# Four operands of the output projection made ahead in place of six, with the loads of that work four to five slots ahead of their use

## The chip, the cores and the metric

One core of a Trainium2 chip. The metric is the device time of one run of the whole kernel in microseconds; the time before is the median of three runs. The profile is one more execution, with its own time.

## The reference

A decoder layer on x of 2048 positions by 1024 channels, in float32, cut to what matters here:

```python
xn = rms_norm(h, ln_g)
proj = jnp.einsum('bsd,de->bse', xn, w_in)              # 6 groups of 1024 columns
b_gate, c_gate, x_conv, g_conv, x_lru, g_lru = jnp.split(proj, splits, axis=-1)
y_conv = headwise_rms_norm(short_conv_mixer(b_gate, c_gate, x_conv, conv_w), 8, conv_out_g) * silu(g_conv)
y_lru = headwise_rms_norm(rg_lru_mixer(x_lru, ...), 16, lru_out_g) * silu(g_lru)
h = h + jnp.einsum('bse,ed->bsd', jnp.concatenate([y_conv, y_lru], -1), w_out)
return rms_norm(h, final_g)
```

The mixers are a short convolution and a gated linear recurrence (two small matrix products for its gates, then a scan over the positions).

## The kernel before

**Steps.** All matrix work is cut into 64 steps (`steps`, L287), numbered n in the text. Steps 0 to 23 are the input projection for the first 1024 positions, steps 24 to 47 the same for the second 1024: eight triples of l (the recurrence's two column groups), a and b (the convolution's four), 128 columns of each group at a time. Steps 48 to 63 are the output projection: `("o", ph, m)`, where ph 0 takes the recurrence's half of the channels and ph 1 the convolution's, and m = 0 to 7 takes 256 positions. Each step is a product of a small operand S and a big operand T, each cut into two by two blocks, by a scheme of seven block products in place of eight (L225 has their order). Every operand block is split into a high part, rounded to fp32r, and a low part, and a product takes high by high, high by low and low by high. So a product is 4 x 3 matmuls of 128 by 128 by 512, and a step is 84 of them. All matmuls are issued in `mm` (L900).

**T and S.** T stays in SBUF for many steps: a set for each half of the positions, and one for each ph (w_out). Steps 24, 48 and 56 begin with a new T; they do six products interleaved by T's parts as these come in, and their seventh product in the next step. S changes with each step. Seven S tiles of 512 KB go round in a pool (`sp`). S is made by `s_plan` (L179) from four raw blocks: four sums on DVE, seven casts on ACT (`hi`, L200), seven subtractions (`lo`), all on DVE from step 24 on. In the first half the results are also stored in `sd`, and the second half loads them instead (`s_loads`, L218): seven loads of 512 KB a step.

**The output projection's S** is z, the mixers' output with its per-head norm: `load_z` (L300) loads four blocks of yd (raw, 256 KB each) and four of the norms' reciprocal roots (zr, 256 KB each by a broadcast; for ph 0 in two halves of 64 partitions, so 12 transfers, for ph 1 8). Four multiplications on DVE follow in later slots. Called for a step itself, zr lies in the tiles u and r of the recurrence; called for the work below, in four more pieces of the raw pool (8 pieces).

**Work made ahead.** z for the first 1024 positions (m = 0 to 3) is known early in the second half, so the generator `jobs` (L363) makes seven operand tiles for some of the steps `(ph, m)` during steps 30 to 47: it loads z, multiplies, and then makes one operand a slot, a cast on ACT (L421) and a subtraction on DVE into a tile of the pool hl (4 buffers), whose store to `so` (512 KB) is asked two slots later. In between it makes T's sums of w_out: `blocks` loads four raw blocks (1 MB), `sums` and `more` combine them on DVE, and four stores (1 MB) to `td` follow; there are eight such sets. When the step comes, `load_next` (L917) finds it in `made` and loads the seven operands from `so`, or else makes them by `s_plan` from `load_z`.

**Order.** Each engine works off its instructions in the order in which the program writes them. There is no scheduler: a slot begins with `tick` (L151), which runs what `at` put off and one piece of `jobs`; then come the loads and preparations (`prep`) for the next step, then the slot's matmuls. `may` (L352) holds the making back in five slots of each a step and when hl is short. Nearly all transfers are asked on SP, in order; a transfer waits for its buffer, and all behind it wait too. At most eight are under way.

**Loads of the steps.** `load_next(n + 2)` stands in slot 3 of a step (L1177), which is four or five slots ahead of the multiplications. In steps that begin with a new T it stands at their end (L1161), after the preparations that load the first five S tiles of step n + 1, and the multiplications come in the first two slots of that step.

Of the kernel before, what the change touches and what calls it, by code (L numbers as in the profile page):

```python
# [38 lines left out]
def hymba_kernel(ctx: ExitStack, tc: tile.TileContext, x, xt, w_in, par, lamc, w_gate, w_out, final_g, out):  # L39
# [27 lines left out]
    def piece(name):  # L67
        return rawp.tile([P, C], F32, tag="raw", name=name)

    def aux(name):  # L70
        return small.tile([P, C], F32, tag="aux", bufs=4, name=name)
# [72 lines left out]
    def at(slots, *fs):  # L144
        if slots == 0:
            for f in fs:
                f()
        else:
            due.append([slots, fs])
# [12 lines left out]
    def tt(out, a, b, op, eng=None):  # L162
        (eng or nc.vector).tensor_tensor(out=out, in0=a, in1=b, op=op)  # L163
# [188 lines left out]
    def may():  # L352
        p = place[0]
        if 8 <= p <= 12:
            return False
        return hlc[0] < (2 if p >= 20 or p <= 2 else 4)

    def w_blocks(t, j):
        k = j + (3 - t) * KT
        return [w_out[(k + i * NB) * P:(k + i * NB + 1) * P, q * C:(q + 1) * C]  # L360
                for i in range(2) for q in range(2)]

    def jobs():  # L363
        tjobs = [(t, j) for t in (2, 3) for j in range(NB)]
        for ph, m in ((0, 0), (0, 1), (1, 0), (1, 1), (0, 2), (0, 3)):
            (a11, a12, a21, a22), fs = load_z(ph, m, False, None)
            yield
            yield
            for f in fs[:2]:
                f()  # L370
            yield
            for f in fs[2:]:
                f()
            yield
            x_ = aux("s3")
            tt(x_, a11, a21, ALU.subtract)
            tt(a21, a21, a22, ALU.add)
            b = {}

            def blocks():  # L380
                if tjobs:
                    b[0] = tjobs.pop(0)
                    b[1] = [piece("traw") for _ in range(4)]
                    for p, src in zip(b[1], w_blocks(*b[0])):
                        nc.sync.dma_start(p, src)

            def sums():
                if b:
                    b11, b12, b21, b22 = b[1]
                    tt(b11, b12, b11, ALU.subtract)  # L390
                    tt(b12, b22, b12, ALU.subtract)

            def more():
                if b:
                    b11, b12, b21, b22 = b[1]
                    tt(b22, b22, b11, ALU.subtract)
                    tt(b21, b21, b22, ALU.subtract)
                    to = td[b[0]]
                    at(1, lambda: [nc.sync.dma_start(to[n], v) for n, v in enumerate((b22, b11, b12, b21))])
                    b.clear()  # L400

            blocks()
            prev = None
            nothing = lambda: None
            items = [(0, a11, lambda: tt(a11, a21, a11, ALU.subtract)), (3, x_, nothing), (2, a21, nothing),
                     (1, a11, nothing), (4, a12, lambda: tt(a12, a12, a11, ALU.subtract)),
                     (6, a22, nothing), (5, a12, nothing)]
            for n, (i, v, after) in enumerate(items):
                if prev:
                    prev()  # L410
                    prev = None
                if n in (1, 5):
                    sums()
                if n in (2, 6):
                    more()
                if n == 4:
                    blocks()
                while not may():
                    yield
                t, = hl_tile("so")  # L420
                nc.scalar.copy(t[:, 0:C], v)  # L421

                def prev(t=t, i=i, v=v, after=after, dst=so[ph, m]):
                    tt(t[:, C:2 * C], v, t[:, 0:C].bitcast(F32), ALU.subtract)
                    after()
                    at(2, lambda: nc.sync.dma_start(
                        dst[i], t.bitcast(F32).rearrange("p (h c) -> p h c", h=2)))
                    at(3, lambda: hl_done(1))

                yield  # L430
            prev()
            made.add((ph, m))
            yield


    class TParts:
# [105 lines left out]
    sums, summed = [None], [0]  # L542
# [374 lines left out]
    def load_next(n, d=2):  # L917
        if n < N:
            Sn[n] = {}
            kind, h, k = steps[n]  # L920
            src = None
            if kind == "o":
                src = so[h, k] if (h, k) in made else None
            elif h == 1 and k > 0:
                src = sd[3 * k + "lab".index(kind)]
            plan[n] = s_loads(src, Sn[n]) if src is not None else s_plan(n, load_s(n, d), Sn[n])

    def prep(n, s):
        if n < N:
            plan[n][s]()  # L930
# [3 lines left out]
    with tc.manual_schedule(engines={ENG.PE, ENG.Activation, ENG.DVE, ENG.Pool, ENG.SP}):  # L934
# [176 lines left out]
        for n in range(PLAIN, N):  # L1111
# [9 lines left out]
            if jm:  # L1121
                bk = {}
                for j in range(NB):
                    place[0] = 2 * j
                    tick()
                    if j < 3:
                        tick()
                    if j == 0:
                        prep(n, 7)
                    if Tq is not None and j < 3:  # L1130
                        Tq.parts((14, 21, 28)[j])
                    elif j == 0:
                        Tp[0].hi(6)
                        Tp[0].lo(6)
                        load_t(2, Tp[2].r)
                    elif j == 1:
                        load_t(3, Tp[3].r)
                    if Tq is None and j < 3:
                        Tp[j + 1].whole()
                    if j == 2:  # L1140
                        load_next(n + 1, 0)
                    if j == 3:
                        prep(n + 1, 0)
                    for i in ORDER[:6]:
                        if j == 0:
                            bk[i] = bank(s=i == 2)
                        mm(bk[i], S_, T, i, j, j == 0, j == NB - 1)
                q1, u2, rr = sm("q1"), sm("u2"), sm("rr")
                nc.scalar.copy(q1, bk[0])
                prep(n + 1, 1)  # L1150
                prep(n + 1, 2)
                tt(u2, bk[1], q1, ALU.add)
                prep(n + 1, 3)
                tt(rr, bk[2], u2, ALU.add)
                tt(u2, bk[3], u2, ALU.add)
                prep(n + 1, 4)
                put(11, bk[4], q1)
                put(22, bk[3], rr)
                put(12, bk[5], rr)
                prep(n + 1, 5)  # L1160
                load_next(n + 2, 1)  # L1161
                pend = (S_, None, put, u2)
                continue
            bk = {}
            for s in range(8 if new or last else 7):
# [43 lines left out]
                elif nx:  # L1209
                    if soon and s == 5:  # L1210
                        Tq = TParts(nx, T2)
# [86 lines left out]
```

## Time and profile before

| | |
|---|---|
| time, median of 3 runs | 1403.29 us (1401.82 to 1404.75) |
| profiled execution | 1404.29 us, of which the span is 1402.2 us |
| granted clock of TensorE, mean | 0.981 |
| moved by the DMA engines | 371.00 MB, mean 265 GB/s |
| so: stores and loads | 42 and 42, of 512 KB each |
| DMA s<-sd, raw<-yd | 147 of 512 KB, 64 of 256 KB |

The span goes from the first instruction to the last; what the run's time has beyond it lies around it. In the views, PE is the matmul engine, PEld its loading of weights, DVE, ACT, POOL the vector, scalar and general engines, SPq the queue of SP. A row of the busy time by stretches has the stretch in us, its length, then for each engine its busy time and (x) instructions, the granted clock (PEclk, 1.00 is full), the share of the DMA engines' time and what they moved. A row of the chain of waits has the start, the length and what was waited for or worked. A row of the list of waits says who waited, at which line, for whom: us in total, times, longest. Rows of groups have busy time and mean ns, then idle time ahead of them.

### The profile page before, as it was taken

How to read it: one execution, taken by the hardware profiler on the slowest of the kernel's cores; microseconds unless marked ns; L12 is line 12 of the kernel's file. 1: busy time of each engine (PE TensorE's matmuls, PEld its weight loads, DVE VectorE, ACT ScalarE, POOL GpSimd, SP SyncE). 2: the span in 40 equal slices, each digit the busy share in tenths (PEclk: the TensorE clock that was granted, in tenths of full speed). 3: DMA queues.
4: the chain of work that ended last, by engine and by line, in shares of the span. 5: the costliest groups of instructions: out<-in, count | busy, mean ns of one | idle time of the engine just before them, and what ended most of it. 6: DMA issues, size and time to landing. Idle time of an engine off the chain costs nothing.

```text
span 1402.2 us, 16765 instructions
## 1 busy us (share of the span) xinstructions
PE 1309.4 (93%) x5612; PEld 1056.3 (75%) x5612; DVE 1071.1 (76%) x1274; ACT 749.3 (53%) x1135; POOL 225.9 (16%) x160
## 2 busy tenths in 40 slices
PE   6989999999999997899998998999998989989997
PEld 5867777787877775678876876787886868867886
DVE  6778888798989889778677787666649447658885
ACT  7475767566565756375563545354556123344443
POOL 2204233233433330101010110101010000000000
PEclk9999999999999998999999999999999999999999
DMA  5147698888988875631899999989878798698643
GB/s 216 30 142 252 255 284 238 288 321 274 337 289 311 307 259 205 230 112 43 292 374 356 389 350 385 343 275 323 286 278 275 286 297 256 220 403 296 216 153 138
DMA packets 166485, 371.00 MB, mean 265 GB/s; under 512 B 18944, under 2 KB 53760, under 8 KB 166400
## 3 DMA queue, kind: packets, MB, share of 16 engines
q1 hardware_dynamic: 166112, 369.63, 76.1%
q8 instruction: 44, 0.72, 0.2%
q14 instruction: 41, 0.34, 0.1%
q10 hardware_dynamic: 288, 0.32, 0.1%
HBM read 224.45 MB, written 145.43 MB: 264 GB/s over the span
## 4 chain that ended last, share of the span: by engine, by line
PE 43%; DMA 19%; DVE 14%; ACT 6%; issue 6%; SPq 2%; POOL 1%; DVEq 0%; ACTq 0%; POOLq 0%
PE bank L900 42%; DMA s<-so 3%; DMA zr<-rsd 3%; DVE s L163 3%; DMA sd<-s 3%; DMA yd<-gl 2%; DVE sums L586 2%; PE gate L680 2%; ACT i L687 2%; ACT r L687 1%; DMA traw<-td 1%; DMA so<-so 1%; DVE u L654 1%; DMA raw<-in_w_in_dram 1%; DMA s<-sd 1%
## 5 line engine op out<-in xcount | busy, mean ns | idle before, releaser
L900 PE MATMUL bank<-th,s 128*128 128x512 f32 x3608 | 1142.2, 395 | 47.8 <-ACT q L1234 12.6
L900 PEld LDWEIGHTS bank<-th,s 128*128 128x128 f32 x3608 | 685.8, 190 | 207.9 <-ACT q L1234 15.6
L900 PE MATMUL bank<-tl,s 128*128 128x512 f32 x1804 | 710.7, 394 | 10.2 <-DVE tl L163 9.9
L900 PEld LDWEIGHTS bank<-tl,s 128*128 128x128 f32 x1804 | 343.0, 190 | 86.4 <-DVE tl L163 15.2
L163 POOL TENSOR_TENSOR s<-raw,s 128x512 fp32r<-128x512 f32 x62 | 110.3, 1791 | 251.3 <-ACT s L200 221.1
L1237 ACT COPY u<-bank 128x512 f32<-128x512 f32 x58 | 34.0, 587 | 168.6 <-PE bank L900 69.6
L200 ACT CAST s<-raw 128x512 fp32r<-128x512 f32 x136 | 82.1, 616 | 64.1 <-PE bank L900 44.2
L163 DVE TENSOR_TENSOR tl<-traw,th 128x512 fp32r<-128x512 f32 x102 | 69.8, 712 | 41.8 <-ACT th L458 24.9
L163 POOL TENSOR_TENSOR gb<-gb,sg 128x1024 f32<-128x1024 f32 x16 | 40.8, 2553 | 351.1 <-ACT sg L613 292.8
L163 DVE TENSOR_TENSOR s<-s,s 128x512 fp32r<-128x512 f32 x102 | 88.9, 871 | 7.9 <-ACT s L200 7.9
L163 DVE TENSOR_TENSOR s<-raw,s 128x512 fp32r<-128x512 f32 (+1 forms) x120 | 85.0, 731 | 10.0 <-ACT s L200 5.3
L1234 ACT COPY q<-bank 128x512 f32<-128x512 f32 x58 | 33.9, 584 | 87.1 <-PE bank L900 70.3
L200 ACT CAST s<-s 128x512 fp32r<-128x512 f32 x102 | 62.8, 616 | 14.6 <-DVE s L163 10.6
L163 DVE TENSOR_TENSOR raw<-raw,zr 128x512 f32<-128x512 f32 x64 | 44.5, 721 | 29.7 <-DMA zr<-rsd 29.6
L654 DVE SCALAR_TENSOR_TENSOR u<-xl,pt,u 128x1024 f32<-128x1024 f32 x48 | 62.3, 1297 | 2.0 <-ACT u L650 1.5
L1240 ACT COPY rr<-bank 128x512 f32<-128x512 f32 x58 | 33.8, 583 | 49.1 <-PE bank L900 49.0
L764 DVE SCALAR_TENSOR_TENSOR t<-p,pt,t 128x1024 f32<-128x1024 f32 x32 | 47.6, 1488 | 8.5 <-ACT t L761 7.7
L163 DVE TENSOR_TENSOR ob<-bank,rr 128x512 f32<-128x512 f32 x18 | 12.2, 689 | 45.2 <-ACT rr L1240 45.2
L163 DVE TENSOR_TENSOR st<-u,st 64x1024 fp32r<-64x1024 f32 x32 | 45.5, 1422 | 1.0
L687 ACT ACTIVATE r<-gate,pt 64x512 f32<-64x512 f32 x64 | 43.8, 684 | 2.3 <-PE gate L680 1.6
L680 PE MATMUL gate<-st,bh 128*128 128x512 f32 x64 | 28.9, 452 | 16.7 <-DVE st L163 6.8
L687 ACT ACTIVATE i<-gate,pt 64x512 f32<-64x512 f32 x64 | 43.8, 684 | 1.1
(159 smaller groups left out, 1279.2 us busy)
## 6 DMA issues: line engine op xcount, KB each, us to landing
sd<-s SPq DMA_DIRECT2D x147, 512.0 KB
s<-sd SPq DMA_DIRECT2D x147, 512.0 KB
raw<-in_w_in_dram SPq DMA_DIRECT2D x108, 256.0 KB
so<-so SPq DMA_DIRECT2D x42, 512.0 KB
s<-so SPq DMA_DIRECT2D x42, 512.0 KB
raw<-yd SPq DMA_DIRECT2D x64, 256.0 KB
traw<-in_w_out_dram SPq DMA_DIRECT2D x56, 256.0 KB
yd<-gl SPq DMA_DIRECT2D x32, 256.0 KB
```

Source lines behind the costliest of these rows:

```text
L163: (eng or nc.vector).tensor_tensor(out=out, in0=a, in1=b, op=op)
L200: nc.scalar.copy(dst[i][0], val(i))
L586: nc.vector.tensor_reduce(out=sums[0][:, kt * R:(kt + 1) * R], in_=y.rearrange("p (a r) -> p r a", r=R), axis=mybir.AxisListType.X, op=ALU ...
L654: nc.vector.scalar_tensor_tensor(out=v["u"], in0=o1[:, 1 + j:1 + j + N2], scalar=lw[j], in1=v["u"], op0=ALU.mult, op1=ALU.add)
L680: nc.tensor.matmul(ps[j], v["gw"][n][:, j, :], v["st"][j][:, sl], start=(n == 0), stop=(n == 1))
L687: nc.scalar.activation(out=g_[hi, sl], in_=v["ps"][j][src], func=AF.Sigmoid, bias=pt[src, bias + k:bias + k + 1])
L764: nc.vector.scalar_tensor_tensor(out=tcur["t"], in0=p[:, 2 + j:2 + j + N2], scalar=cw[j], in1=tcur["t"], op0=ALU.mult, op1=ALU.add)
L900: nc.tensor.matmul(bank, a[:, js], b, start=start and n == 0, stop=stop and n == 2, skip_group_check=more)
L1234: nc.scalar.copy(q1, bk["A"])
L1237: nc.scalar.copy(u2, bk["A"])
L1240: nc.scalar.copy(rr, bk["A"])
```

## The change

Three edits. `jobs` makes four steps' operands, (0, 0), (0, 1), (1, 0) and (1, 1); (0, 2) and (0, 3), which are steps 50 and 51, are no longer in `made`, so `load_next` makes them from `load_z`. Inside a job the first multiplications come four slots after the loads, not two, and a set of w_out is loaded at the job's start and again at its end, each at least four slots ahead of its sums, where it was mostly one or two. And in steps 48 and 56 the load for step n + 2 is asked in the slot of T's last part (j == 3), ahead of that slot's matmuls.

```diff
-        for ph, m in ((0, 0), (0, 1), (1, 0), (1, 1), (0, 2), (0, 3)):
+        for ph, m in ((0, 0), (0, 1), (1, 0), (1, 1)):
             (a11, a12, a21, a22), fs = load_z(ph, m, False, None)
-            yield
-            yield
+            yield from (None,) * 4
             for f in fs[:2]:
                 f()
...
-                if n in (1, 5):
+                if n == 4:
                     sums()
-                if n in (2, 6):
+                if n == 5:
                     more()
-                if n == 4:
-                    blocks()
...
             made.add((ph, m))
             yield
+            blocks()
+            yield from (None,) * 4
+            sums()
+            yield
+            more()
+            yield from (None,) * 2
...
                     if j == 3:
                         prep(n + 1, 0)
+                        if Tq is not None:
+                            load_next(n + 2, 1)
...
-                load_next(n + 2, 1)
+                if Tq is None:
+                    load_next(n + 2, 1)
```

The changed kernel's lines stand three to six lines further down than those of the kernel before (L421 is L418 there, L1234 is L1240).

How the rows move, first on ACT, from the end of step 33 into step 34 (q is the copy that frees the bank of a step's first product, `so<-raw` a cast of the work made ahead). Before:

```order
L1240 COPY rr<-bank 128x512
L421 CAST so<-raw 128x512 x2
L743 COPY xl<-bank 128x512
L650 ACTIVATE u<-xl,pt 128x1024
L421 CAST so<-raw 128x512
L1234 COPY q_6379<-bank 128x512
L605 ACTIVATE t<-t 128x1024
```

and now:

```order
L1246 COPY rr<-bank 128x512
L746 COPY xl<-bank 128x512
L653 ACTIVATE u<-xl,pt 128x1024
L1240 COPY q_6324<-bank 128x512
L608 ACTIVATE t<-t 128x1024
```

Here three casts have gone: the second job now begins some slots later.

On SP at the end of step 48 (traw is the last part of w_out for this T, so01 the operands of step 49, yd1 and rsd0 the z and norms of step 50). Before:

```order
L450 DMA traw_8811<-td23_129 128x512
L221 DMA s_8873<-so01_119 128x1024
L221 DMA s_8875<-so01_119 128x1024
L221 DMA s_8878<-so01_119 128x1024
L221 DMA s_8882<-so01_119 128x1024
L221 DMA s_8887<-so01_119 128x1024
```

and now:

```order
L453 DMA traw_8697<-td23_129 128x512
L313 DMA raw_8737<-yd1_85 128x512
L318 DMA zr_8741<-rsd0_88 64x512
L320 DMA zr_8741<-rsd0_88 64x512
L313 DMA raw_8738<-yd1_85 128x512
```

Three more such groups follow, and then the five loads of so01; of step 50's so loads none is left.

On SP at the end of step 56 (so11 is step 57, yd1 and rsd0 step 58). Before:

```order
L221 DMA s_10204<-so11_123 128x1024
L221 DMA s_10211<-so11_123 128x1024
L313 DMA raw_10213<-yd1_85 128x512
L316 DMA zr_10217<-rsd0_88 128x512
L313 DMA raw_10214<-yd1_85 128x512
L316 DMA zr_10217<-rsd0_88 128x512
L313 DMA raw_10215<-yd1_85 128x512
L316 DMA zr_10222<-rsd0_88 128x512
L313 DMA raw_10216<-yd1_85 128x512
L316 DMA zr_10222<-rsd0_88 128x512
L221 DMA s_10232<-so11_123 128x1024
```

and now:

```order
L453 DMA traw_10089<-td33_133 128x512
L313 DMA raw_10129<-yd1_85 128x512
L316 DMA zr_10133<-rsd0_88 128x512
L313 DMA raw_10130<-yd1_85 128x512
L316 DMA zr_10133<-rsd0_88 128x512
L313 DMA raw_10131<-yd1_85 128x512
L316 DMA zr_10138<-rsd0_88 128x512
L313 DMA raw_10132<-yd1_85 128x512
L316 DMA zr_10138<-rsd0_88 128x512
L221 DMA s_10165<-so11_123 128x1024
L221 DMA s_10167<-so11_123 128x1024
```

The eight loads for step 58 have moved from behind five of step 57's loads to ahead of them.

## Prediction

> **What bounds the kernel now.** I read the page first, then the busy time by stretches cut at the first matmul of each step, then the chain of waits inside the long stretches.
>
> ```profile
> span 1402.2 us, 16765 instructions
> PE 1309.4 (93%) x5612; PEld 1056.3 (75%) x5612; DVE 1071.1 (76%) x1274; ACT 749.3 (53%) x1135; POOL 225.9 (16%) x160
> GB/s 216 30 142 252 255 284 238 288 321 274 337 289 311 307 259 205 230 112 43 292 374 356 389 350 385 343 275 323 286 278 275 286 297 256 220 403 296 216 153 138
> ```
>
> PE is the bound, and the change leaves its work alone. So only time in which PE waits, or runs at half clock, can be won or lost. The profiled execution took 1404.29 us: the span and 2.1 us around it. It is 1.0 us above the median of 1403.29. The transfers are busiest in slices 20 to 25 (343 to 389 GB/s), where operands of the output projection are made ahead. One row there for each triple of steps l, a, b; the first row is the last triple before that work starts.
>
> ```profile
> core 0: us, PE busy (x) PEld busy (x) DVE busy (x) ACT busy (x) POOL busy (x), PEclk, DMA share, GB/s
> 615.00:674.60 59.60, 59.38 (x262) 48.69 (x261) 49.72 (x55) 37.41 (x53) 6.63 (x4) 1.00 0.23 72
> 674.60:735.70 61.10, 60.14 (x262) 48.45 (x260) 44.18 (x51) 31.31 (x43) 5.92 (x4) 1.00 0.99 353
> 735.70:804.30 68.60, 62.96 (x262) 50.36 (x261) 50.28 (x59) 31.28 (x44) 6.82 (x4) 0.95 0.99 374
> 804.30:872.90 68.60, 62.62 (x261) 49.80 (x260) 53.72 (x61) 33.18 (x47) 5.91 (x4) 0.95 0.99 363
> 872.90:936.40 63.50, 59.90 (x261) 48.56 (x260) 41.66 (x49) 31.18 (x43) 5.92 (x4) 1.00 0.91 317
> 936.40:997.20 60.80, 59.70 (x262) 48.68 (x262) 39.38 (x45) 31.39 (x43) 5.93 (x4) 1.00 0.89 295
> 997.20:1059.60 62.40, 62.06 (x273) 50.86 (x272) 35.84 (x41) 32.96 (x46) 6.83 (x4) 1.00 0.85 294
> ```
>
> An undisturbed triple takes 59.6 us. The six take 385.0. Six times 59.6, plus 2.7 for the 12 matmuls that the last one has more, is 360.3. So **24.7 us are lost in this stretch**, and 18.0 of them in the second and third triple, where the DMA share is 0.99 and the clock 0.95. How they are lost shows in the chain of waits in the second triple, step 34, and in the list of waits for the whole stretch:
>
> ```profile
> 757.71 7.51 DMA so<-so
> 765.25 0.62 ACT so L421
> 765.86 0.49 ACT q L1234
> 766.40 16.55 PE bank L900 x60
> ```
>
> ```profile
> DVE gl L163 <- DMA yd<-gl: 32.2, 6, 8.0
> ACT so L421 <- DMA so<-so: 23.6, 5, 8.4
> ```
>
> A store of a made operand takes 7.5 us to land, since the transfers are full. ACT's next cast into that buffer waits for it, and behind the cast on ACT stands the copy q that frees the bank PE needs. DVE waits in the same way for stores of the mixers' output (yd). After such a wait the clock is halved for some time:
>
> ```profile
> 765.20:772.00 6.80, 5.60 (x13) 4.49 (x14) 4.63 (x6) 2.06 (x3) 0.00 (x0) 0.50 1.02 400
> 1139.50:1144.30 4.80, 4.72 (x14) 3.72 (x15) 3.79 (x6) 1.19 (x3) 0.00 (x0) 0.64 1.02 418
> ```
>
> The second row costs 0.36 x 4.8 = 1.7 us; that is my price for one halving. Then the output projection, steps 48 to 52 and 56 to 58:
>
> ```profile
> 1059.60:1085.90 26.30, 19.53 (x74) 14.23 (x73) 24.78 (x30) 16.27 (x26) 3.26 (x1) 0.94 0.80 275
> 1085.90:1105.50 19.60, 19.60 (x88) 16.27 (x89) 11.85 (x13) 4.23 (x7) 0.00 (x0) 1.00 1.01 392
> 1105.50:1125.20 19.70, 19.24 (x85) 15.59 (x84) 3.84 (x4) 2.77 (x5) 0.00 (x0) 1.00 0.57 183
> 1125.20:1152.20 27.00, 21.37 (x84) 16.85 (x85) 11.43 (x16) 4.73 (x9) 0.00 (x0) 0.94 0.93 297
> 1152.20:1171.20 19.00, 19.00 (x85) 15.76 (x84) 16.34 (x26) 6.40 (x11) 0.00 (x0) 1.00 0.96 277
> 1231.10:1255.50 24.40, 17.62 (x74) 12.90 (x72) 13.15 (x20) 10.40 (x17) 0.00 (x0) 1.00 1.04 403
> 1255.50:1277.70 22.20, 21.08 (x85) 16.92 (x86) 18.68 (x29) 7.46 (x14) 0.00 (x0) 0.92 0.98 349
> 1277.70:1296.70 19.00, 19.00 (x85) 15.76 (x84) 16.13 (x25) 8.98 (x17) 0.00 (x0) 1.00 0.74 267
> ```
>
> A step of 84 matmuls needs 19.0 us. Steps 52 and 58, whose operands are made on the spot from yd, run at 19.0 without a wait. Step 51, which reads operands made ahead, takes 27.0.
>
> **Part 1: four jobs, and their loads spread.** By the code a job moves 2.1 MB in (yd and the norms), 3.7 MB of operands out, and 1 MB in and 1 MB out for each block of w_out. Before, all eight blocks and nearly four of the six jobs fall into the first three triples; after, five blocks and two and a half jobs. Adding all transfers by the slot in which they are asked gives 73.2 MB for these three triples (24.2, 23.2, 25.8), that is 410 GB/s over 3 x 59.6 us. No row here moves over 418, and a whole step at a share of 1.04 moves 403: a backlog builds up. After, the same three have 60.1 MB (336 GB/s), and the six have 19.0, 20.0, 21.1, 21.6, 19.0, 17.4 MB; the fullest is 363 GB/s. So the backlog no longer grows from triple to triple, and the waits for so and yd, which are waits for landings, shrink to what one burst of seven operands causes. What is left I read from two triples of before. The first, at 353 GB/s and without an old backlog, loses 1.5 us; the fifth, at 295, loses 1.2 on one job alone. Four jobs at some 1.2 us each leave 4.8. **Term A = 4.8 - 24.7 = -20 us.** Bounds: 24.7 if nothing waits; 12 if half of the loss came from the bursts alone, which stay as dense as they were. ACT loses 14 casts and DVE 30 operations in this stretch, two jobs' worth; they had room (in the rows above DVE works 36 to 54 us of 60 and more), so I cost that at nothing.
>
> **Part 2: steps 50 and 51 are made on the spot.** The work comes back in steps 49 and 50. A step's worth is on DVE 4 multiplications, 4 sums and 7 low parts, on ACT 7 casts:
>
> ```profile
> L163 DVE TENSOR_TENSOR raw<-raw,zr 128x512 f32<-128x512 f32 x4 | 2.6, 683 | 0.0
> L200 ACT CAST s<-raw 128x512 fp32r<-128x512 f32 x4 | 2.4, 618 | 1.9 <-PE bank L900 1.9
> ```
>
> 15 x 0.68 = 10.2 us on DVE and 7 x 0.62 = 4.3 on ACT. DVE then has 11.85 + 10.2 = 22 us in step 49 and 14 in step 50, where PE needs 19: step 49 would be 3 over if it stayed at 19.6, but by the next part it grows, and DVE has step 50 to catch up. I cost this at nothing; without that cover it is 3 us. What it removes is the wait in step 51:
>
> ```profile
> 1131.62 7.92 DMA s<-so
> ```
>
> That load of an operand of step 51 stands on SP behind the loads for step 52, which wait for the 24 small stores of the norms; PE waits for it until 1139.5. Without so loads in steps 50 and 51 there is nothing to wait for. What is late next are the norms for step 52's own operands: their multiplications already held DVE up here. I take 19.7 in place of 27.0: **-7.3** (bounds -7.9 and -2, if DVE's wait keeps PE back).
>
> **Part 3: one load is asked for ahead of others.** At steps 48 and 56 the 12 (or 8) transfers of step n+2's operand now stand on SP between the last part of w_out and the five so loads of step n+1, whose first is what PE waits for:
>
> ```profile
> 1077.40 0.38 SPq L450 DMA_DIRECT2D traw<-td  x1
> 1081.44 3.07 SPq L221 DMA_DIRECT2D s<-so  x5
> ```
>
> ```profile
> 1081.44 4.32 DMA s<-so
> 1085.89 11.15 PE bank L900 x48
> ```
>
> ```profile
> 1247.52 0.32 SPq L450 DMA_DIRECT2D traw<-td  x1
> 1249.64 3.10 SPq L221 DMA_DIRECT2D s<-so  x5
> 1252.83 0.38 SPq L313 DMA_DIRECT2D raw<-yd  x1
> ```
>
> ```profile
> 1252.42 8.07 DMA s<-so
> 1260.51 5.33 DMA zr<-rsd
> 1265.93 0.70 DVE raw L163
> ```
>
> In both places PE starts the step when the first so load lands (1085.9 and 1255.5). At 1252 the fifth so load lands at 1260.5, and the last of the yd and norm loads, asked next, 5.4 us later, at 1265.9: transfers land in the order in which they are asked. So the 2.1 MB cost 5.4 us when the engines are full, and put in front they delay the so loads by that.
>
> The Trainium skill says so too ("DMA: Bandwidth & Descriptors", Queues, rings and completion order): on each DMA engine the descriptors of one issuing queue are consumed in ring order, though later ones may finish first. The landings above agree; by that rule the second edit must delay the so loads, and the sum is the one below; if it did not hold, the sum would be that of rival 1.
>
> At step 49 the DMA share was 0.80 in the step before, so part may fall into gaps; but the pieces that the loads go to are freed only as DVE splits the last parts of w_out, in this same step, so little can start early. I take 5.4 for both. The wait at step 49 then becomes some 6 us, no shorter than those that a halved clock follows above: 1.7 more. **Step 49: +7** (3 to 9).
>
> At step 57 the halving is paid already (0.08 x 22.2 = 1.8). The rest of its 3.2 us over 19.0, 1.4, is PE waiting behind DVE's multiplication at 1265.9; with the loads in front that goes. **Step 57: 5.4 - 1.4 = +4** (0 to +7).
>
> **Sum.** -20 - 7.3 + 7 + 4 = -16.3 us: 1404.3 - 16.3 = 1388.0 for the profiled execution, **1387 us** against the median.
>
> **The rivals.**
> 1. The loads in front cost nothing, since the engines take them beside the others or in gaps. For it: a share of 0.80 before step 49. Against it: 1.04 and 403 GB/s before step 57. Then -20 - 7.3 - 1.4 = -28.7: 1375. Chance 0.15.
> 2. The stretch ahead stays half disturbed: a burst of seven stores with the loads of three steps is as dense as before, and every cast of it can block ACT. For it: 1.2 us lost in the fifth triple at only 295 GB/s. Against it: the bursts of the fourth and fifth triple, the same in kind, lose 5.1 together where the second and third lose 18. Then -12 - 7.3 + 7 + 4 = -8.3: 1395. Chance 0.2.
> 3. Slower: the queue in front of steps 49 and 57. The place is the head of each of these two steps, the price what the loads take at the poorer rate of step 52 (277 GB/s at a share of 0.96: 2.1 MB in 7.3 us) and a halving each, 9 us; and step 51 keeps its 27.0 because the multiplications for step 52 still wait behind the stores of the norms. That is +18, and it decides as soon as term A gives under 18. With A at -12 it is +6: 1409. For it: DVE's place in line at 1265.9. Against it: PE reaches step 51 some 7 us later than now while those stores are asked at most as late. Chance 0.06.
> 4. The change does little: the waits for so and yd come from the order of the casts on ACT, not from full transfers, and term A is only a few us that the loads in front eat up: 1403. Against it: the triple without this work runs at 59.6. Chance 0.04.
>
> My forecast has the remaining 0.55. A measurement of this kernel can tell 0.2% (2.8 us) from no change. Faster: the forecast, rivals 1 and 2, 0.9; within 0.2%: 0.04; slower: 0.06. The terms' bounds reach from -24.7 - 7.9 + 3 + 0 = -30 to -12 - 2 + 9 + 7 = +2; with one in ten left out at each end, 1376 to 1398.
>
> **What would show each step.** Term A: no triple between step 30 and 47 over 62 us (65 for the last), DMA share under 0.95, ACT's wait for so under 6 us. Part 2: step 51 under 21 us, DVE over 20 us in step 49. Part 3: step 49 at 25 us or more with a granted clock under 1, step 57 at 25 or more, and no DVE wait for zr there. I am wrong in the main if the triples keep their 68 us, or if steps 49 and 57 stay at 20 and 22.

## The result and the profile after

| | before | after |
|---|---|---|
| median | 1403.45 us (1401.82 to 1404.75, 4 runs) | 1391.68 us (1390.34 to 1392.37, 4 runs) |
| profiled execution | 1404.29 us, span 1402.2 | 1391.93 us, span 1390.0 |
| mean granted clock | 0.981 | 0.977 |
| moved by the DMA engines | 371.00 MB | 356.32 MB |

The ratio is 0.9913, with a 95% interval of 0.9892 to 0.9933: faster by 11.8 us, where 16.3 were forecast. The head of the page of after:

```profile
span 1390.0 us, 16694 instructions
PE 1305.4 (94%) x5612; PEld 1058.0 (76%) x5612; DVE 1069.3 (77%) x1274; ACT 748.9 (54%) x1135; POOL 225.7 (16%) x160
```

Where the 12.2 us of the span went is read from the busy time by stretches, cut at the first matmul of each step or triple as before. First the stretch of the made-ahead work, steps 30 to 47:

```profile
675.00:734.50 59.50, 59.28 (x261) 48.70 (x260) 40.64 (x47) 30.63 (x43) 6.54 (x4) 1.00 0.88 297
734.50:798.80 64.30, 61.53 (x262) 49.73 (x261) 41.35 (x47) 30.11 (x41) 6.86 (x4) 0.97 0.93 332
798.80:858.40 59.60, 59.26 (x261) 48.69 (x260) 42.22 (x49) 29.99 (x41) 6.62 (x4) 1.00 0.98 353
858.40:918.10 59.70, 59.36 (x261) 48.72 (x261) 45.83 (x50) 30.11 (x41) 5.91 (x4) 1.00 0.99 363
918.10:979.30 61.20, 59.88 (x262) 48.60 (x261) 44.01 (x46) 31.27 (x42) 5.88 (x4) 1.00 0.91 317
979.30:1041.70 62.40, 62.06 (x273) 50.86 (x272) 33.42 (x36) 31.41 (x44) 6.08 (x4) 1.00 0.77 253
```

They sum to 366.7 us, where before had 385.0: -18.3. The second triple still loses 4.7 us and the fifth 1.6, against the 59.6 of an undisturbed one. The loss does not follow the rate: the third and fourth triples have a DMA share of 0.98 and 0.99 and lose nothing. In the list of waits for this stretch of after, the casts' wait for so (23.6 us before) is gone, while DVE's wait for yd is as long as it was (32.2). The cast of L421 stands at L418 here, three lines further up and not further down, and the matmuls of L900 at L903:

```profile
DVE gl L163 <- DMA yd<-gl: 32.4, 4, 8.6
...
ACT so L418 <- DVE raw L163: 4.7, 1, 4.7
```

What is left in the second triple stands in step 34, and the chain of waits there begins with that wait for yd:

```profile
743.79 9.38 DMA yd<-gl
753.29 0.69 DVE gl L163
...
767.41 5.35 DMA s<-sd
772.90 3.24 PE bank L903 x9
```

DVE stands still until a store of the mixers' output has landed. Its sums of w_out come late by that, SP cannot ask for their stores earlier, and the loads of z and of the next S stand behind those stores on SP; PE waits for the last of them.

Then the output projection, steps 48 to 51, 56 and 57:

```profile
1041.70:1076.80 35.10, 19.56 (x74) 14.22 (x73) 32.27 (x40) 16.27 (x26) 3.28 (x1) 0.87 0.88 278
1076.80:1098.50 21.70, 21.70 (x88) 17.77 (x89) 11.31 (x17) 6.89 (x11) 0.00 (x0) 0.90 0.95 320
1098.50:1117.60 19.10, 19.10 (x86) 15.80 (x85) 12.58 (x19) 6.29 (x11) 0.00 (x0) 1.00 0.49 138
1117.60:1136.60 19.00, 19.00 (x85) 15.73 (x84) 16.01 (x25) 6.39 (x11) 0.00 (x0) 1.00 0.90 266
1215.50:1244.80 29.30, 19.78 (x73) 15.22 (x72) 18.33 (x28) 10.42 (x17) 0.00 (x0) 0.83 1.04 399
1244.80:1265.70 20.90, 20.89 (x85) 17.11 (x86) 13.21 (x20) 7.36 (x14) 0.00 (x0) 0.91 0.86 321
```

Cut at the first matmul of a step, the wait ahead of that matmul stands in the row of the step before: the wait for step 49's operands is in step 48's row. So the pairs are compared. Steps 48 and 49: 45.9 us before, 56.8 now, +10.9. Steps 50 and 51: 46.7 before, 38.1 now, -8.6. Steps 56 and 57: 46.6 before, 50.2 now, +3.6. With -18.3, and 0.4 us more ahead of step 30, that makes -12.0 of the 12.2.

The chain of waits at the head of step 49 in after shows the order in which the change put things on SP: a load of the norms for step 50, then the so load, then PE.

```profile
1063.14 7.71 DMA zr<-rsd
1070.92 5.71 DMA s<-so
1076.76 13.26 PE bank L903 x48
```

And at step 57:

```profile
1231.63 7.20 DMA raw<-yd
1238.89 5.78 DMA s<-so
```

### The profile page after: what moved, and what is told of

The parts are those of the page before. It is cut to its first block, busy times and chain, and to the rows that moved or that the text cites. A ratio compares the mean times of both kernels' runs of the same rounds, so it can differ in the third digit from the quotient of the medians.

```text
span 1390.0 us, 16694 instructions
## 1 busy us (share of the span) xinstructions
PE 1305.4 (94%) x5612; PEld 1058.0 (76%) x5612; DVE 1069.3 (77%) x1274; ACT 748.9 (54%) x1135; POOL 225.7 (16%) x160
## 2 busy tenths in 40 slices
DMA packets 162453, 356.32 MB, mean 256 GB/s; under 512 B 18496, under 2 KB 53312, under 8 KB 162368
## 4 chain that ended last, share of the span: by engine, by line
PE 47%; DVE 16%; DMA 14%; ACT 7%; issue 6%; SPq 1%; POOL 1%; DVEq 0%; ACTq 0%; POOLq 0%
PE bank L903 46%; DVE s L163 3%; DMA sd<-s 2%; DVE sums L589 2%; DMA raw<-in_w_in_dram 2%; DMA yd<-gl 2%; ACT i L690 1%; ACT r L690 1%; DMA traw<-in_w_out_dram 1%; PE gate L683 1%; DMA xcol<-rsx 1%; DMA s<-sd 1%; DVE tl L163 1%; DMA traw<-td 1%; DVE r L717 1%
## 5 line engine op out<-in xcount | busy, mean ns | idle before, releaser
L903 PE MATMUL bank<-th,s 128*128 128x512 f32 x3608 | 1139.4, 394 | 43.4 <-DMA s<-so 16.0
L903 PEld LDWEIGHTS bank<-th,s 128*128 128x128 f32 x3608 | 685.9, 190 | 198.4 <-issue 21.7
L903 PE MATMUL bank<-tl,s 128*128 128x512 f32 x1804 | 711.0, 394 | 10.1 <-DVE tl L163 9.8
L903 PEld LDWEIGHTS bank<-tl,s 128*128 128x128 f32 x1804 | 343.1, 190 | 86.3 <-DVE tl L163 14.8
L200 ACT CAST s<-raw 128x512 fp32r<-128x512 f32 x144 | 87.1, 616 | 73.5 <-PE bank L903 54.7
L163 DVE TENSOR_TENSOR s<-raw,s 128x512 fp32r<-128x512 f32 (+1 forms) x130 | 91.6, 726 | 9.9 <-ACT s L200 5.3
L163 DVE TENSOR_TENSOR s<-s,s 128x512 fp32r<-128x512 f32 x108 | 93.2, 863 | 6.4 <-ACT s L200 6.4
L1240 ACT COPY q<-bank 128x512 f32<-128x512 f32 x58 | 33.9, 584 | 100.1 <-PE bank L903 87.4
L200 ACT CAST s<-s 128x512 fp32r<-128x512 f32 x108 | 66.6, 616 | 14.1 <-DVE s L163 10.3
L163 DVE TENSOR_TENSOR st<-u,st 64x1024 fp32r<-64x1024 f32 x32 | 48.5, 1517 | 1.0
L163 DVE TENSOR_TENSOR raw<-raw,zr 128x512 f32<-128x512 f32 x64 | 41.4, 681 | 7.5 <-DMA zr<-rsd 7.4
L163 DVE TENSOR_TENSOR ob<-bank,rr 128x512 f32<-128x512 f32 x18 | 12.2, 689 | 44.1 <-ACT rr L1246 44.1
L163 POOL TENSOR_TENSOR gl<-gl,sg 128x1024 f32<-128x1024 f32 x16 | 39.8, 2485 | 22.3 <-ACT sg L616 22.2
```

Of the source, the lines that this page charges most:

```text
L200: nc.scalar.copy(dst[i][0], val(i))
L903: nc.tensor.matmul(bank, a[:, js], b, start=start and n == 0, stop=stop and n == 2, skip_group_check=more)
L1240: nc.scalar.copy(q1, bk["A"])
```

## The experiments

Each ratio is to the kernel before, with its 95% interval, from five rounds beside it on the same chip.

**1. The loads at the end again.**

```diff
                     if j == 3:
                         prep(n + 1, 0)
-                        if Tq is not None:
-                            load_next(n + 2, 1)
...
                 prep(n + 1, 5)
-                if Tq is None:
-                    load_next(n + 2, 1)
+                load_next(n + 2, 1)
```

> The changed kernel with its third edit undone: in steps 48 and 56 the load for step n + 2 stands at the step's end again, behind the five so loads. Theory (transfers land in the order in which they are asked, so the loads in front delay what PE waits for): PE's wait before step 49 falls from 8.2 us to about 1 to 2.5, that before step 57 from 6.8 to about 2.5; steps 48 and 49 together fall from 56.8 us to about 47, steps 56 and 57 from 50.2 to about 47; the time from 1391.7 to about 1379. Rival (the engines are full there anyway, or the multiplications for step 50 now wait for their late blocks and hold PE up in step 49 as long): 1388 to 1392.

Measured: 1386.33 us, 0.9879 (0.9842 to 0.9915). The time lies between the theory's and the rival's. Steps 56 and 57 took 24.5 + 22.2 = 46.7 us, as the theory said. Steps 48 and 49 did not fall as it said:

```profile
1041.30:1068.00 26.70, 20.95 (x74) 15.49 (x72) 24.80 (x30) 16.18 (x26) 3.25 (x1) 0.87 0.80 264
1068.00:1096.40 28.40, 21.75 (x89) 17.50 (x89) 17.79 (x25) 6.89 (x12) 0.00 (x0) 0.88 1.01 290
```

Together 55.1, only 1.7 less than in after. The wait ahead of step 49 went (step 48 is back at 26.7), and another came inside step 49. PE's row in the timeline of this kernel shows where it stands (in brackets the idle time before the row, and who ended it):

```profile
1082.73 0.42 PE L562 MATMUL norm_ps<-rt,sel 128*96 128x256 f32 x1 [3.65 <-ACT rt L555]
1086.15 0.96 PE L562 MATMUL norm_ps<-rt,sel 128*96 128x256 f32 x3 [3.00 <-DVE rt L163]
```

and DVE's rows show why:

```profile
1077.52 0.69 DVE L163 TENSOR_TENSOR raw<-raw,zr 128x512 f32<-128x512 f32 x1 [5.05 <-DMA zr<-rsd]
1079.56 0.69 DVE L163 TENSOR_TENSOR raw<-raw,zr 128x512 f32<-128x512 f32 x1 [1.35 <-DMA zr<-rsd]
1080.17 1.90 DVE L589 TRANSPOSE_TENSOR_REDUCE sums<-t 128x32 f32<-128x1024 f32 x1
```

The multiplications for step 50 wait on DVE for their norms; the last head's sums stand behind them; the norm's four small matmuls wait for the sums' low part, and step 49's other matmuls stand behind those on PE. So the price of step 50's loads at this place does not go with their order: whoever comes second waits. My theory held for step 57 and fell for step 49.

**2. The third edit alone, on the kernel before.**

```diff
                 prep(n + 1, 5)
-                load_next(n + 2, 1)
+                if Tq is None:
+                    load_next(n + 2, 1)
```

and `load_next(n + 2, 1)` at j == 3, as in after.

> The kernel before with the third edit alone. Since step 50's operands are still made ahead, the edit moves only step 58's eight loads, in front of step 57's so loads. Theory: PE's wait before step 57 grows by 4 to 5 us, the wait for the norms in step 57 goes, steps 56 and 57 together go from 46.6 us to about 50, the time from 1403.4 to about 1407. Rival (the loads go in gaps and cost nothing): 1402 to 1403.5.

Measured: 1403.97 us beside 1400.89, 1.0019 (0.9997 to 1.0042): the time alone tells no difference for certain. The profile does: steps 56 and 57 took 29.6 + 20.5 = 50.1 us, 3.5 more than the 46.6 of before, and PE's wait there is

```profile
PE bank L900 <- DMA s<-so: 7.7, 1, 7.7
```

5.3 us more than the 2.4 of before. The theory holds at step 57.

**3. Four jobs, spaced and loaded as before.**

```diff
-        for ph, m in ((0, 0), (0, 1), (1, 0), (1, 1), (0, 2), (0, 3)):
+        for ph, m in ((0, 0), (0, 1), (1, 0), (1, 1)):
```

> The kernel before with the list of jobs cut to four and nothing else: spacing and place of the loads as before. It tells the number of jobs from their spacing. Theory (full transfers make the stretch slow, and the first four jobs with their eight sets of w_out are as dense as before until step 41): about 20 us of the 24.7 us lost in steps 30 to 47 stay, step 51 falls from 27 to about 19.5, and the time is about 1391 to 1395. Rival (fewer jobs do it): the stretch falls to about 367 us and the time to about 1377 to 1380.

Measured: 1398.56 us, 0.9986 (0.9962 to 1.0010): no difference from before is shown by the time, and the theory's 1391 to 1395 was missed. The second and third triple, and step 49:

```profile
731.30:799.20 67.90, 61.53 (x262) 49.72 (x261) 48.05 (x59) 31.24 (x44) 7.20 (x4) 0.97 1.00 373
799.20:868.10 68.90, 63.50 (x262) 50.19 (x261) 53.79 (x62) 33.27 (x47) 5.90 (x4) 0.95 1.00 369
...
1076.20:1105.10 28.90, 22.11 (x88) 17.83 (x89) 19.13 (x27) 7.16 (x12) 0.00 (x0) 0.88 1.05 292
```

Steps 30 to 47 took 379.6 us in the profile: 5.4 of the 18.3 come from the number of jobs, most of it in the fourth and fifth triple, which are at 59.7 and 59.6; the rest comes from the spacing. Step 51 is at 19.0, and step 49 rose from 19.6 to 28.9, with the loads at the end, as in experiment 1. So fewer jobs by themselves won 8.6 us in steps 50 and 51 and lost 9.3 in step 49, which the theory had left out.

**4. The load between the so loads.**

```diff
                 prep(n + 1, 2)
+                if Tq is not None:
+                    load_next(n + 2, 1)
                 tt(u2, bk[1], q1, ALU.add)
```

in place of the same call at j == 3.

> The changed kernel with the load for step n + 2 in steps 48 and 56 put behind the first two so loads of step n + 1 and ahead of the other three. Theory (order of landing): PE's waits before steps 49 and 57 are as short as with the load at the end, and the blocks still come some 4 us sooner for the multiplications: steps 48 and 49 about 47 us, 56 and 57 about 46, the time about 1378, as fast as with the load at the end or up to 2 us faster. Rival (what fills the engines counts, not the order): 1386 or more.

Measured: 1381.01 us, 0.9849 (0.9812 to 0.9886). The pairs:

```profile
1035.60:1062.50 26.90, 19.48 (x74) 14.18 (x72) 25.03 (x31) 16.21 (x26) 3.28 (x1) 0.94 0.81 271
1062.50:1089.40 26.90, 22.76 (x89) 18.34 (x90) 15.94 (x22) 6.88 (x11) 0.00 (x0) 0.87 1.00 290
...
1207.40:1231.60 24.20, 18.89 (x73) 14.25 (x72) 13.16 (x20) 10.43 (x17) 0.00 (x0) 0.92 1.04 402
1231.60:1252.20 20.60, 20.60 (x84) 16.92 (x85) 18.27 (x29) 7.35 (x14) 0.00 (x0) 0.92 1.04 401
```

The time lies between the theory's and the rival's. Steps 56 and 57 take 44.8, 5.4 less than in after: here order pays. Steps 48 and 49 take 53.8, not 47: now PE waits 4.1 us for the third so load, which stands behind the twelve. The expectation was right at one place and wrong at the other.

**5. The norm's matmuls later.** Experiment 1's kernel and

```diff
-            at(1, lambda: head_norms(h))
+            at(4 if h else 1, lambda: head_norms(h))
```

> The changed kernel with the loads for step n + 2 at the end of steps 48 and 56 again (as in e1), and with the second half's norm (the copy rt, its low part, the four small matmuls and what follows) three slots later. Theory, formed after e1: the wait that came in place of the one for so is PE's 7 us in front of the norm's matmuls in step 49, since on DVE the sums and the low part for them stand behind step 50's multiplications, which wait for late norms. Then step 49 falls from e1's 28.5 us to 19 to 21 and the time to about 1378. Rival: DVE is late with step 50's operands in any case, so PE waits for them at the head of step 50 instead, and steps 49 and 50 together stay at 45 to 48 us: 1384 to 1387.

Measured: 1391.51 us, 0.9930 (0.9910 to 0.9951). That is above both ranges. Step 49 took 28.9 (28.4 in experiment 1), and step 51 rose to 25.1, since the norms for step 52 now came later. The norm's matmuls had only been first in a row: with them gone, PE waits for ACT's copy u of a bank, ACT for DVE, and DVE for the same multiplications:

```profile
ACT u L1240 <- DVE ob L163: 8.1, 1, 8.1
PEld bank L903 <- ACT u L1240: 7.0, 1, 7.0
```

This theory was wrong; the rival was right that DVE is late in any case, though the wait stands inside step 49 and not at the head of step 50. What stops the step is DVE, standing still for loads.

**6. A fifth job, so that step 50 is made ahead again.**

```diff
-        for ph, m in ((0, 0), (0, 1), (1, 0), (1, 1)):
+        for ph, m in ((0, 0), (0, 1), (1, 0), (1, 1), (0, 2)):
```

> The changed kernel with a fifth job, (0, 2), at the end of the list: step 50's operands are made ahead again, spaced as the others, step 51's stay on the spot. Theory: what costs 10 us in steps 48 and 49 is not the place of step 50's loads but that there are such loads at all (12 transfers at some 250 GB/s, wherever they stand); without them steps 48 and 49 go from 56.8 us back to about 46, steps 50 and 51 stay near 19 to 20 each, the fifth job costs 0 to 3 us in steps 43 to 46, and the time is 1381 to 1385. Rival (the engines are behind at the end of step 48 in any case, or step 51 gets the wait that step 49 had): 1389 to 1394.

Measured: 1390.22 us (1385.54 to 1392.63), 0.9922 (0.9899 to 0.9944), in the rival's range. The fifth job cost nothing in steps 30 to 47 (366.0 us). Steps 48 and 49 are back at 26.5 + 19.7 = 46.2, as the theory said, but step 50 takes 26.6. The chain of waits in step 50 begins with a so load of 8 us and goes on through the small stores of the norms; SP's row of these and the chain's second so load:

```profile
1085.87 13.13 SPq L575 DMA_DIRECT2D rsd<-hn  x24
1099.09 0.34 SPq L221 DMA_DIRECT2D s<-so  x1
```

The last two operands of step 50 stand behind 24 small stores. It is the wait that step 51 had before, one step earlier. So the sum of steps 48 to 51 was 92.6 before, 94.9 after, and 93.3, 93.3, 92.9 and 92.9 in experiments 1, 3, 4 and 6: waits at five places, of one size.

**7. More bytes, same order.** Behind each store of a made operand and each group of w_out's stores, in after:

```diff
+    def extra():
+        nc.sync.dma_start(spare.pop(0), x[0:P, :].rearrange("p (h c) -> p h c", h=2))
```

> The changed kernel with 36 added transfers of 512 KB from DRAM to DRAM, one behind each store of a made operand and one behind each group of w_out's stores: about 12 MB more in the first three triples of the stretch, some 400 GB/s in place of 336; no operation of ACT, DVE or PE is added or moved, and nobody reads what is written. Theory of term A (full transfers let stores land late, and ACT and DVE wait for their buffers): the waits for so and yd come back, steps 30 to 47 go from 366.7 to 378 to 390 us, the time to 1403 to 1415. Rival (the waits came from the order of the casts and the spacing, not from full transfers): the stretch stays at 366 to 370 us and the time at 1390 to 1395.

Measured: 1416.12 us, 1.0110 (1.0084 to 1.0135); steps 30 to 47 took 392.5 us, 25.8 more than after. The time is the theory's; the waits are not:

```profile
DVE gl L163 <- DMA yd<-gl: 32.6, 5, 10.9
...
PE bank L908 <- DMA s<-sd: 15.1, 4, 7.7
```

No cast waits for so. PE waits for its own operands, loaded from sd, more than it did in after (2.8 us). So more transfers can cost as much, but by another wait than the one that the change removed. Each added transfer also takes one of the eight places under way, so bytes and places are not told apart here.

**8. Five jobs, and the load for step 58 between.** Experiments 4 and 6 together.

> Five spaced jobs (as e6), and in step 56 the load for step 58 between the second and the third so load (as e4). Theory: e6's time less 4 to 5 us at steps 56 and 57: 1377 to 1380. Rival (as in e6): 1385 or more.

Measured: 1382.61 us, 0.9873 (0.9851 to 0.9895). Steps 56 and 57 took 24.1 + 20.7 = 44.8 where experiment 6 had 51.3; step 50 kept its wait (25.1). The time is between the theory's and the rival's, and the profile has the theory's place.

**9. The same, with the second half's small stores on POOL's queue.**

```diff
-                        nc.sync.dma_start(
+                        (nc.gpsimd if h else nc.sync).dma_start(
                             rsd[h][i, b, k0:k0 + KT, :]...
```

> The kernel of e8 with the 24 small stores of the second half's norms asked on POOL's queue, not on SP's. Theory, formed after e6: the 6 to 7 us that came back in step 50 are two so loads that stand on SP behind these stores (13 us of issuing); off SP, step 50 falls from 25.1 to 19 to 20 us, steps 48 to 51 from 92.2 to 85 to 87, and the time from e8's 1382.6 to 1374 to 1377. Rival (some 93 us for steps 48 to 51 is what the transfers or DVE allow in every order, and the wait only moves on): 1380 to 1384.

Measured: 1375.45 us (1371.39 to 1379.95), 0.9822 (0.9799 to 0.9845). Steps 48 to 51:

```profile
1034.50:1060.10 25.60, 19.40 (x73) 14.06 (x72) 24.10 (x29) 15.46 (x26) 3.27 (x1) 0.93 0.80 273
1060.10:1079.80 19.70, 19.69 (x89) 16.34 (x90) 10.82 (x14) 4.95 (x7) 0.00 (x0) 1.00 1.02 338
1079.80:1099.30 19.50, 19.50 (x85) 15.58 (x84) 11.33 (x15) 5.26 (x9) 11.07 (x19) 1.00 0.92 318
1099.30:1121.00 21.70, 19.31 (x85) 15.69 (x84) 15.98 (x25) 6.29 (x11) 3.17 (x6) 1.00 0.86 245
```

86.5 us. The theory holds. This version has the lowest ratio of all, and its interval lies wholly below that of after (0.9892 to 0.9933); it overlaps that of experiment 4.

**10. The kernel before with these stores on POOL's queue, and nothing else.**

> The kernel before with the same stores on POOL's queue and nothing else. Part 2 of the prediction put step 51's 8 us to so loads that stand on SP behind these stores. Theory: step 51 falls from 27.0 to 19 to 20.5 us with six jobs and without the change, and the time from 1403 to about 1395.5. Rival (the so load is late for another reason, or the wait moves into step 52): 1401 to 1404.

Measured: 1394.22 us, 0.9953 (0.9936 to 0.9969). Step 51, 27.0 before:

```profile
1123.90:1143.00 19.10, 19.10 (x86) 15.80 (x85) 9.22 (x13) 5.26 (x9) 0.00 (x0) 1.00 0.97 337
```

One line takes away the wait that two jobs were given up for. Part 2's account of that wait is shown. Six jobs with the change's spacing and these stores on POOL's queue were not run together.

**11. Half of the loads in front.** In after, the norms of step 50 are loaded for its first block and used for all four, so that step computes with the wrong norms.

```diff
+                if once:
+                    fs.append(lambda zz=zz: tt(zz, zz, once[0], ALU.mult))
+                    continue
+                if zr and (h, m) == (0, 2):
+                    once.append(zq)
```

> The changed kernel, in which step 50's norms are loaded for the first of its four blocks alone and used for all four: 6 of the 12 transfers in front of step 49's so loads, 0.75 of the 2.1 MB, are left out, and step 50 computes with the wrong norms. It sizes the price of these loads. If they cost by their bytes at 400 GB/s, as the prediction had it, the wait before step 49 falls by 1.9 us from 8.2, and the time to about 1389.5. If the broadcast norms are the dear part (the engines were full at 220 to 256 GB/s while these 12 landed), it falls by 4 to 6 us, to 2 to 4, the halved clock goes too, and the time is 1384 to 1387.

Measured: 1385.36 us, 0.9893 (0.9873 to 0.9914). PE's longest wait for an operand in steps 48 and 49, 8.2 us in after:

```profile
PE bank L909 <- DMA s<-so: 3.3, 1, 3.3
```

0.75 MB less took 4.9 us off, where 400 GB/s would give 1.9. The halved clock stayed (0.93 and 0.87 in the rows of steps 48 and 49), against the expectation. The dear price fits better, by one profile of each kernel; the times alone do not tell the two apart, since the interval overlaps that of after. Whether these loads are dear by being broadcast or by being many was not separated.

**12. Fewer bytes, same order.** The kernel before, with the stores of w_out's sums cut to a quarter of their columns and the rest written from x in steps 27 to 29, so that the output projection computes with other numbers.

```diff
-                    at(1, lambda: [nc.sync.dma_start(to[n], v) for ...])
+                    at(1, lambda: [nc.sync.dma_start(to[n][:, 0:P], v[:, 0:P]) for ...])
```

> The kernel before, in the same order on every engine, but each store of w_out's sums in the stretch carries a quarter of its columns (64 KB in place of 256); the other three quarters are written from x, in 32 transfers during steps 27 to 29, where the engines are at 72 GB/s, so the output projection computes with other numbers. Some 6 MB leave the stretch, 67 MB in place of 73 in its first three triples (375 GB/s in place of 410). If full transfers are what makes ACT's casts wait for the stores of so, as term A had it, that wait falls from 23.6 us to under 10, steps 30 to 47 from 385.0 us to 368 to 374, and the time to 1387 to 1393. Rival (the waits come from how dense the casts stand; e7 lost its time with none of them): the wait for so stays at 18 us or more, the stretch at 380 us or more, the time at 1399 or more.

Measured: 1398.96 us, 0.9971 (0.9952 to 0.9990). The second and third triple:

```profile
735.10:803.40 68.30, 62.33 (x261) 50.31 (x260) 49.71 (x59) 31.18 (x44) 6.96 (x4) 0.95 0.99 345
803.40:871.90 68.50, 63.08 (x262) 50.50 (x261) 52.60 (x62) 33.28 (x47) 5.91 (x4) 0.95 0.95 335
```

and the casts' wait:

```profile
ACT so L421 <- DMA so<-so: 19.3, 5, 8.2
```

At 345 and 335 GB/s these two triples still take 68.3 and 68.5 us; before had 68.6 each at 374 and 363, and after runs at 59.6 and 59.7 with 353 and 363. The whole stretch gave 3.5 us (381.5). The time falls on the rival's bound, and the wait and the stretch are the rival's: what the casts wait for does not go away with these bytes. The engines stayed busy for 0.99 and 0.95 of the time, so idle engines were not tried.

## Why the prediction was right, and where it was not

**The sum.** -20 - 7.3 + 7 + 4 = -16.3 were forecast, -12.2 measured in the span. The sign and the range were right, the size came out a quarter smaller, and each of the four terms has its sign. Reasons behind three of the terms were not right, so that the total fits is in part luck.

**Term A: the size right, the cause wrong.** -20 was forecast and -18.3 came, most of it in the second and third triple. The step that failed is "So the backlog no longer grows from triple to triple, and the waits for so and yd, which are waits for landings, shrink". The wait for yd did not shrink (32.2 and 32.4), and the loss that is left in step 34 goes back to it. The DMA share did not fall under 0.95 in the third and fourth triple, and they lose nothing. Experiments 12 and 7 show both halves: bytes taken out of the dense order give 3.5 us and leave the casts' wait at 19.3, and bytes put into the spaced order do not bring that wait back. Experiment 3 shows that it is the spacing: with four jobs in the dense order the two triples keep 67.9 and 68.9.

How the spacing does it is read from the traces and argued, not tested part by part. In step 34 it is the order on ACT: before, casts of the second job stood between the end of step 33 and the copy q of step 34, and after none does. A store's landing took 7.51 us in the row of step 34 before and 7.10 in experiment 12, so a cast that needs the buffer again within that time waits, and the copy behind it with it. In the third triple, step 37, a cast waits for so as well (8.4 us), but PE's longest wait in the list for before is another one:

```profile
PE gate L680 <- DVE st L163: 3.8, 1, 3.8
```

It goes back over DVE to the third job's four multiplications, the first of them two slots behind their loads. The last of their norms was asked by SP at 839.0 us and landed at 845.8, and the operands of the recurrence's gates (st) stand behind these multiplications on DVE. In after they come four slots behind their loads. Which part of the spacing wins how much was not separated. So rival 4 was right that full transfers alone do not make these waits, and right in part with "the order of the casts on ACT"; its conclusion was wrong, since the change moves that order too.

**What is left of the stretch** is 6.4 us, where 4.8 were forecast: 4.7 in step 34 and 1.6 in the fifth triple, not some 1.2 in each of four jobs. Its size is partly chance: in eight kernels with the same order up to there, step 34 took between 21.9 and 26.6 us.

**Part 2: the gain right, the cover not there.** Step 51 fell by 8.0 (forecast 7.3), and by the wait that was named, as experiment 10 shows. What failed is "I cost this at nothing; without that cover it is 3 us". The added work on DVE is short, but four of its operations wait for loads, and on DVE everything for step 49 stands behind them. In experiments 1 and 3 that is 8.8 and 9.3 us in step 49, more than step 51 had won. The list of what to look for named DVE's busy time; it should have asked what DVE waits for, and who waits behind it.

**Part 3: at step 57 right, at step 49 in the wrong account.** The prediction's "second edit" there is the third one, the load at j == 3. +4 was forecast for step 57 and +3.6 came; experiments 1 and 2 give 3.5 each, and the wait of DVE for the norms went. The rule of the Trainium skill that was weighed there ("DMA: Bandwidth & Descriptors", Queues, rings and completion order: on each DMA engine one queue's descriptors are consumed in ring order) agrees with this, and with the 5.4 us that experiment 4 won by the order alone. At steps 48 and 49 +7 was forecast and +10.9 came. The size is short because the 2.1 MB were priced at 5.4 us, at the rate of step 56. Here, while they land, the engines are full at less:

```profile
1063.50:1070.50 7.00, 5.07 (x16) 3.68 (x14) 4.72 (x8) 2.31 (x4) 0.00 (x0) 0.76 1.06 299
1070.50:1076.50 6.00, 0.00 (x0) 0.00 (x0) 6.00 (x8) 0.00 (x0) 0.00 (x0) 0.54 1.04 294
```

The wait grew by 7.1 us (1.05 to 8.19), which is near the 7.3 that rival 3 took, and experiment 11 agrees with the dear price. Of the rest, 2.1 us are the lower clock in step 49 (PE busy for 21.70 us, 19.60 before), and 1.6 a wait of PE in step 48 for a part of T from ACT (2.06 us, 0.46 before). And the account: the third edit itself costs 1.7 us there (56.8 less 55.1), not 7, since without it the same loads cost 8.8 inside step 49. What costs is that step 50 is made on the spot.

**The rivals.** 1 (loads in front cost nothing) and 2 (half disturbed) are out by the rows above. 3, slower, needed term A under 18 and step 51 at 27; neither came, the first by 0.3 us only; its price for the loads was the better one at step 49.

**What to look for.** Of six triples one is over its bound (64.3 against 62). Step 51 is under 21. DVE's busy time in step 49 is 11.3 and not over 20: two of the multiplications fall into the wait ahead of it, and more of the added work falls into step 50 (12.6, where before had 3.8). Steps 49 and 57 are not 25 or more by themselves: the waits stand in the rows of 48 and 56, a slip in how the forecast was put. No wait of DVE for zr is left in steps 56 and 57.

## What to carry to other kernels

Before an operation is moved onto an engine, ask not how long it takes but what it waits for, and what stands behind it there: four multiplications of 0.7 us cost 9 us in step 49 because their data were late and the work behind them on DVE waited too. A row that reads "full share" does not prove that bytes are the cause; take bytes out in the same order, and put bytes in, before believing it. And when a wait of one size turns up in one place after another as things are moved, look for what all of them queue behind: here, moving 24 small stores off SP won 6.7 us by itself.

## What the runs showed of the hardware

- A full share of the DMA engines is not a rate. At a share of 1.04 they moved 399 GB/s in step 56 of after and 294 while the norms for step 50 landed. Without 0.75 MB of those norms the wait was 4.9 us shorter (experiment 11).
- Half clock can last longer than the waits ahead of it. In step 56 of after PE waited 1.0 us and, 0.9 us later, 1.7 us, and the stretch behind ran at half clock throughout:

```profile
1222.60:1228.00 5.40, 5.40 (x14) 4.23 (x13) 1.35 (x2) 1.58 (x3) 0.00 (x0) 0.50 1.03 413
```

In before PE waited 1.2 and 1.7 us at the same place, and the clock was 1.00 in the whole of step 56. So the length of a wait alone does not decide it, and what does stays open.

- 24 small stores held SP for 8.4 us in experiment 5 and for 13.1 in experiment 6, against 0.3 to 0.4 us for the issue of a load of 512 KB. On POOL's queue they took longer (14.2 us of POOL's time in step 50 of experiment 10), but PE did not wait in step 51.
- On one chip the kernel before spread from 1392.82 to 1409.93 us, more than in the runs of the first chip (1401.82 to 1404.75); its four runs there could not have shown how far it goes.
